# Differential attention's keys as pairs of the front, and query swaps by transfers inside SBUF, in a two-layer trunk step

## The chip, the cores and the metric

The kernel runs on one core of one Trainium2 chip. The metric is the device time of one execution in microseconds; the median of several runs counts. The profile is taken from one more execution.

## The reference

One inference step of a two-layer trunk for 128 prompt tokens and 512 sample tokens (640 columns in the kernel), model width 2048, in float32. Each layer: RMSNorm, shift and scale from a condition, one wide input projection whose column groups feed two mixers and their gates, one output projection, gated residual.

```python
def odd_mixer(h, w_in, w_out, cqn, ckn, c_lam, c_on, dqn, dkn, lam_init, ctx=None, rope=None):
    cq, ck, cv, cg, dq, dk, dv, dg = split_cols(h @ w_in, ODD_SPLIT)
    ...
    cq = rms_norm(cq.reshape(b, t, 2, C_HEADS, HEAD_DIM).transpose(0, 2, 3, 1, 4), cqn)
    ck = rms_norm(ck.reshape(b, t, 2, C_HEADS, HEAD_DIM).transpose(0, 2, 3, 1, 4), ckn)
    ...
    if ctx is None:
        ...
        new = (ck, cv, k_d, v_d)
    else:
        cos, sin = rope
        cq = apply_rope(cq, cos, sin)
        q_d = apply_rope(q_d, cos, sin)
        ck_all = jnp.concatenate([ctx[0], apply_rope(ck, cos, sin)], axis=3)
        ...
    o1 = attend(cq[:, 0][:, :, None], ck_all[:, 0], cv_all)[:, :, 0]
    o2 = attend(cq[:, 1][:, :, None], ck_all[:, 1], cv_all)[:, :, 0]
    o_c = rms_norm(o1 - lam.astype(o1.dtype) * o2, c_on) * (1.0 - lam_init)
    y_c = o_c.transpose(0, 2, 1, 3).reshape(b, t, C_W) * jax.nn.silu(cg)
    y_d = merge_heads(attend(q_d, dk_all, dv_all)) * jax.nn.silu(dg)
    return jnp.concatenate([y_c, y_d], axis=-1) @ w_out, new
```

Layer 1 (`odd_mixer`) has 4 heads of differential attention (C: two queries and two keys a head, 8 query and 8 key columns of 128, values of 256) and 8 query heads on 2 key heads of grouped attention (D). A key is normed by its row's RMS, scaled by a gain, and rotated by its position where it belongs to a sample token; 256 cached context keys go ahead of it. The normed prompt keys are an output as well. Layer 0 has banded grouped attention and a short convolution.

## The kernel before, in words

**Columns and products.** The input is held transposed: 16 tiles of 128 features x 640 tokens (`hs`), each as a high and a low part (float32r). A *column tile* is 128 columns of a weight matrix against all 640 tokens. Weights are loaded in quarters (4 x 128 rows, `load_raw`, on SP's queue), split into a high part by ScalarE and a low part by VectorE (`split_w`), and multiplied three times (high x high, high x low, low x high), in two halves of 320 tokens: 16 x 3 x 2 = 96 matmuls of 320 columns a tile.

**Tiles with work between them (`run_tiles`).** `slot` is called after each quarter, `pace_attn` after each half quarter. `prep` is a list of generators that finish a tile (each is advanced once a slot); `attn` is a queue of attention generators, of which only the first is advanced, by `steps / 2` at each of the eight calls in a tile (`brisk` holds `steps` by tile). `fill` is the modulation's product on VectorE, advanced `rate` times a slot (`FILL1`). Weights are loaded five quarters ahead and split three ahead (`RAW_AHEAD`, `SPLIT_AHEAD`). The program is written in this order; the order on each engine is made by the framework when it builds the kernel, and can differ (in the trace the scores of a step stand in the midst of a half quarter's matmuls).

**Pairs (`run_pairs`).** Two column tiles are multiplied together in seven products M1 to M7 in place of eight, from sums of weight blocks (VectorE: `sx`, `sf`) and of input blocks that are made once (`forms`): 7 x 8 x 3 = 168 matmuls of 320 columns a pair, and 14 weight splits of 128x512, where two plain tiles have 192 and 8. `begin` is called at a pair's start, `done` when a half of a tile is finished, `tail` in the last pair.

**Layer 1.** Its *front* (`project` with `h1_maker`, from about 1086 us to 1432 us) makes 14 gates, the 2 key tiles of D and the 10 value tiles of both mixers: six as plain tiles, twenty as ten pairs. Gates, keys and values go to HBM (`gdram`, `kdram`, `vdram`); values are transposed to rows ahead of that (`value_rows`), the two keys go raw. Then the pool `mid` is closed and `odd` opened, and a `run_tiles` of 26 tiles follows (the *mixers*, to about 2060 us): 8 queries of D, then for each of the four heads of C two queries and two keys, then two late gates. Attention runs between these tiles. `q_gen` finishes a query: it evicts it with its gain, copies four blocks of 32 partitions to swapped places (`qsw`, L751, on ScalarE), multiplies by cosines and sines, and sums squares on TensorE. `k_gen` finishes a key: transposes to rows, sums of squares (`junk`, L694), gain (L696, L699), the power -0.5 on GpSimd (L704), scaling (L707), rotation (L714 to L719), an output transfer, transposes back (L656) and splits, after `drain(attn)`. `keys_first` does it for D's keys, from their transfer back (`kx`, L684).

**One step of attention.** `pair_gen` (D) and `diff_gen` (C) alternate for each block of 128 queries: scores of the first query or map into PSUM (`S`, one buffer, L847 to L849), row maximum on VectorE (L809), its scaling (L811) and the exponential (L816) on ScalarE, then the second; transposes of the probabilities (L835), their splits, and the product with the values some steps later. A head of C has 15 steps. Keys and values have one buffer each, queries two.

Of the kernel before, what the change touches and what calls it, by code (L numbers as in the profile page):

```python
# [11 lines left out]
F32 = mybir.dt.float32  # L12
F32R = mybir.dt.float32r
# [7 lines left out]
P = 128  # L21
# [30 lines left out]
FILL1 = 0.85  # L52
# [4 lines left out]
def trunk_kernel(ctx: ExitStack, tc: tile.TileContext, I: dict, O: dict):  # L57
# [286 lines left out]
    prep, attn = [], []  # L344

# [324 lines left out]
    def k_gen(ap, pp, tag, src, gain, new_out, vals=None, then=None):  # L670

        vx = []

        def v_in(j):
            vx.append(ap.tile([P, 5, P], F32, tag="stg", name="vx", bufs=2))
            nc.sync.dma_start(vx[j].rearrange("p b f -> p (b f)"), vals[1][j])

        raw = ap.tile([P, 2, P], F32, tag="ctxk", name="ctxk", bufs=1)
        nc.sync.dma_start(raw, src.rearrange("(c p) d -> p c d", p=P))
        if isinstance(pp, tuple):  # L680
            x = stage(ap, pp)
        else:
            x = ap.tile([P, NT], F32, tag="stg", name="kx", bufs=2)
            nc.sync.dma_start(x, pp)  # L684
        if vals:
            v_in(0)
        yield
        ss = small.tile([P, 5], F32, tag="ss", name="ss")
        kg = ap.tile([P, 5, P], F32, tag="rp", name="kg", bufs=3)
        junk = ap.tile([P, P * st["sets"]], BF16, tag="junk", name="junk", bufs=1)[:, 0:P]  # L690
# [9 lines left out]
        if vals:  # L700
            v_in(1)
# [3 lines left out]
        yield  # L705
# [3 lines left out]
        m1 = ap.tile([P, 4, P], F32, tag="rp", name="m1", bufs=3)  # L709
        m2 = ap.tile([P, 4, P], F32, tag="rp", name="m2", bufs=3)  # L710
        x = kg[:, 0:4, :].rearrange("p b (a h f) -> p (b a) h f", a=2, h=2)
        y = m1.rearrange("p b (a h f) -> p (b a) h f", a=2, h=2)
        z = m2.rearrange("p b (a h f) -> p (b a) h f", a=2, h=2)
        V.tensor_mul(y, x, cosR[:, :, None, :].to_broadcast([P, 8, 2, 32]))  # L714
        yield
        V.scalar_tensor_tensor(out=z[:, :, 0, :], in0=x[:, :, 1, :], scalar=-1.0, in1=sinR,
                               op0=ALU.mult, op1=ALU.mult)
        V.tensor_mul(z[:, :, 1, :], x[:, :, 0, :], sinR)
        V.tensor_add(m1, m1, m2)  # L719
        yield  # L720
        drain(attn)
# [5 lines left out]
        split(hi[:, 0:CTX], lo[:, 0:CTX], t[:, 0:CTX])  # L727
        t = to_rows(lambda b: kg[:, b, :], False)
# [3 lines left out]
        if vals:  # L732
            yield
            hi, lo = st["v"] = tuple(ap.tile([P, 7, 2 * P], F32R, tag=t, name=t) for t in ("vh", "vl"))
            ctx_v(ap, vals[0], hi, lo, 2 * P)
            for j in range(2):
                cols = slice(j * P, (j + 1) * P)
                split(hi[:, 2:7, cols], lo[:, 2:7, cols], vx[j])
        if then:
            attn.append(then())  # L740


    def q_gen(ap, pp, tag, gain, then=None, wait=True):
# [5 lines left out]
        sw = ap.tile([P, NS], F32, tag="rp", name="qsw", bufs=3)  # L749
        for d in range(4):  # L750
            A.copy(sw[32 * d:32 * d + 32, :], x[32 * (d ^ 1):32 * (d ^ 1) + 32, 0:NS])  # L751
        yield
        m = ap.tile([P, NS], F32, tag="rp", name="qm", bufs=3)
        V.tensor_mul(m, x[:, 0:NS], cosT)
        V.tensor_mul(sw, sw, sinT)
        V.tensor_add(m, m, sw)
# [6 lines left out]
        if wait:  # L763
            yield
        t = psT()
# [108 lines left out]
    def pair_gen(ap, width, k, v, qs, banded, begin, emit, done, sinks):  # L874
# [38 lines left out]
        for u in range(7):  # L913
            if u >= 2:
                weigh(u - 2, [0, 2])
                groups(u - 2, [4])
            if u < 5:
                score(u, 0)
            yield
            if u >= 2 and len(plan(u - 2)[4]) > 4:  # L920
                weigh(u - 2, [4])
            if u < 5:
                score(u, 1)
            if 1 <= u < 6:
                groups(u - 1, [0, 2])
            if u < 6:
                yield
        done()
# [24 lines left out]
    kdram = [dram.tile([P, NT], F32, name=f"kd{k}") for k in range(2)]  # L953
# [4 lines left out]
    st = {"sets": 1}  # L958
# [580 lines left out]
    def odd_start():  # L1539
        ap = pools["cur"]  # L1540
        lam4 = ap.tile([P, 4, P], F32, tag="rp", name="lam4", bufs=3)
        nc.sync.dma_start(lam4, I["c_lambda"][0].rearrange("a d -> (a d)").partition_broadcast(P)
                          .rearrange("p (a d) -> p a d", a=4))
        lp = ap.tile([P, 2, P], F32, tag="rp", name="lp", bufs=3)
# [17 lines left out]
    def diff_gen(ap, h, v, kq):  # L1562
# [66 lines left out]
        for u in range(8):  # L1629
            if u >= 3:  # L1630
                out(u - 3)
            if 2 <= u < 7:
                weigh(u - 2)
            if u < 5:
                score(u, 0)
            if u == 7:
                break
            yield
            if u >= 2:
                norm(u - 2)  # L1640
            if u < 5:
                score(u, 1)
            if 1 <= u < 6:
                groups(u - 1)
            yield
# [31 lines left out]

    def key_out(j):
        x = xr_tile("kx")

        def put(t, sl, src):
            A.copy(x[:, sl], src)
            if (j, "k") in half_done:
                nc.gpsimd.dma_start(kdram[j], x)
            half_done.add((j, "k"))
        return put
# [7 lines left out]

    def front_begin(p):
        for t in range(2):
            n = N_FRONT + 2 * p + t
            m = n - len(FRONT)
            outs[t] = gate_out(n) if m < 0 else key_out(m) if m < 2 else value_out((m - 4) if m > 3 else m + 6)

    def front_done(p, t, h, src):
        outs[t](("sq", "acc")[t], HV[h][1], src)

    def front_tail(name):

        if name == "M7":
# [8 lines left out]
    project(I["od_w_in"][0], [(OD["cg"] + i * P) if i < 8 else OD["dg"] + (i - 8) * P for i in FRONT]  # L1715
            + [OD[n] + i * P for n, m in (("dk", 2), ("dv", 2), ("cv", 8)) for i in range(m)], N_FRONT, h1_maker,
            front_job, front_begin, front_done, front_tail, by_half=True)
    nc.sync.dma_start(tables, I["k_tables"])
    close("mid")
    open_pool("odd")  # L1720
    odd_start()
# [10 lines left out]
    st["sets"] = 2  # L1732
# [8 lines left out]
    def keys_first():  # L1741
        for kv in range(2):
            yield from k_job(f"k{kv}", I["cache_d_k"][0, 0, kv], "d_k_norm", O["new_d_k"][0, 0, kv])(kdram[kv])

    def in_twos(g):
        while next(g, DONE) is not DONE and next(g, DONE) is not DONE:
            yield

    def behind(g):
        yield  # L1750
        yield from g

    keys = keys_first()
    next(keys)
    prep.append(behind(in_twos(keys)))
    for h in range(4):
        for m in range(2):
            jobs.append((OD["cq"] + (m * 4 + h) * P, q_job(f"q{m}", "c_q_norm")))
        for m in range(2):
            more = (None, diff_then(h)) if m else ((I["cache_c_v"][0, 0, h], vdram[2 * h:2 * h + 2]),)  # L1760
            jobs.append((OD["ck"] + (m * 4 + h) * P,
                         k_job(f"k{m}", I["cache_c_k"][0, 0, m, h], "c_k_norm", O["new_c_k"][0, 0, m, h], *more)))

    brisk = {len(jobs): 1.75, len(jobs) + 1: 1.75}
    brisk.update((i, 1.6 if i < 11 else 1.1) for i in range(2, len(jobs)))
    for i in (4, 5):
        jobs.append((OD["cg"] + i * P, very_late_gate(i, (("rp", 3), ("stg", 2), ("rp", 3)))))
# [5 lines left out]
    def y1_maker(k):  # L1773
# [6 lines left out]
        else:  # L1780

            tag, n = (("q0h", 2), ("q0l", 2), ("q1h", 2), ("q1l", 2))[k] if k < 4 else (("rp", 3), ("stg", 2))[k % 2]
# [100 lines left out]
```

## Time and profile before

| | |
|---|---|
| median of 3 runs | 2266.32 us (2265.68 to 2266.66) |
| the profiled execution's own time | 2267.87 us |
| its span, first to last instruction | 2265.9 us |
| mean granted TensorE clock | 0.996 |
| TensorE matmul busy / weight load busy | 2221.5 us (98%) / 2148.4 us (95%) |
| VectorE / ScalarE / GpSimd busy | 1693.1 (75%) / 1167.9 (52%) / 223.5 us (10%) |

The profile's page gives busy times over the whole span. Matmuls are pipelined, so two records overlap and a mean of about 310 ns for a 320-column matmul is twice the time between two of them; windows with their instruction counts give that time. In rows of windows the columns are: stretch, its length, then busy us and (x instructions) of TensorE's matmuls, its weight loads, VectorE, ScalarE and GpSimd, the granted clock, the DMA share, and GB/s. In rows of groups: line, engine, operation, tiles written and read, shapes, count, then busy us, mean ns of one, idle time before and what ended it.

### The profile page before, as it was taken

To read this page: it belongs to the slowest core of one execution; us is meant where nothing else is said; L and a number is where in the kernel's file an instruction comes from. 1 tells how busy PE (TensorE), PEld (TensorE's weight loads), DVE (VectorE), ACT (ScalarE), POOL (GpSimd) and SP (SyncE) were. 2 spreads that over 40 slices of the span, in tenths; PEclk is the share of its full clock that TensorE was granted. 3 is DMA by queue.
4 is the path that set the end of the run, shared out by engine and by line. 5 is a ranking of instruction groups with operands and counts; after the bars stand their busy time and mean duration, and the time that the engine had idled before them with its cause. 6 is when DMAs were issued, how large, how long until landed. Compare 5 with 4: busy or idle time off the path is not lost.

```text
span 2265.9 us, 41110 instructions
## 1 busy us (share of the span) xinstructions
PE 2221.5 (98%) x15660; PEld 2148.4 (95%) x15660; DVE 1693.1 (75%) x2981; ACT 1167.9 (52%) x2473; POOL 223.5 (10%) x341
## 2 busy tenths in 40 slices
PE   7999999999999999999999999999999999999999
PEld 5889999999999999999999999899999999999999
DVE  4659898988888978877876666585766786576765
ACT  4335554645344445444744445577775666664443
POOL 2221101000100100000200000100001111111010
PEclk9999999999999999999999999999999999999999
DMA  9985556565453426753763333432424343246541
GB/s 357 330 287 173 160 167 198 173 188 161 154 156 113 150 85 219 218 148 106 261 200 108 117 110 112 151 103 70 124 84 140 96 132 111 83 134 224 166 135 45
DMA packets 377189, 354.03 MB, mean 156 GB/s; under 512 B 17170, under 2 KB 324848, under 8 KB 376480
## 3 DMA queue, kind: packets, MB, share of 16 engines
q1 hardware_dynamic: 360272, 291.07, 42.1%
q0 software_dynamic: 15856, 58.11, 7.3%
q8 instruction: 123, 2.02, 0.4%
q10 hardware_dynamic: 864, 2.23, 0.3%
q14 instruction: 74, 0.61, 0.1%
HBM read 307.17 MB, written 44.17 MB: 155 GB/s over the span
## 4 chain that ended last, share of the span: by engine, by line
PE 83%; DMA 4%; issue 4%; ACT 3%; DVE 3%; POOL 1%; SPq 1%; POOLq 0%; DVEq 0%; ACTq 0%
PE pq L626 10%; PE pq L628 10%; PE pq L627 10%; PE pa L332 6%; PE pa L333 6%; PE pb L332 6%; PE pa L334 6%; PE pb L333 6%; PE pb L334 6%; PE T L835 2%; PE S L847 2%; PE S L849 1%; PE S L848 1%; PE T L178 1%; DMA ada<-in_ada_w 1%
## 5 line engine op out<-in xcount | busy, mean ns | idle before, releaser
L297 ACT ACTIVATE wh<-raw 128x512 fp32r<-128x512 f32 (+1 forms) x388 | 233.2, 602 | 343.4 <-PE pb L333 227.4
L332 PE MATMUL pa<-h,wh 128*128 128x320 f32 x1152 | 367.7, 319 | 0.6 <-DVE sum L425 0.4
L332 PE MATMUL pb<-h,wh 128*128 128x320 f32 x1152 | 360.4, 313 | 0.9 <-ACT h L297 0.9
L333 PE MATMUL pa<-h,wh 128*128 128x320 f32 x1152 | 359.4, 312 | 0.9 <-DVE h L298 0.9
L334 PE MATMUL pa<-h,wl 128*128 128x320 f32 x1152 | 358.3, 311 | 0.0
L333 PE MATMUL pb<-h,wh 128*128 128x320 f32 x1152 | 357.8, 311 | 0.0
L334 PE MATMUL pb<-h,wl 128*128 128x320 f32 x1152 | 357.8, 311 | 0.0
L298 DVE TENSOR_TENSOR wl<-raw,wh 128x512 fp32r<-128x512 f32 (+1 forms) x388 | 253.5, 654 | 110.7 <-ACT wh L297 99.7
L626 PE MATMUL pq<-h,wh 128*128 128x320 f32 x960 | 297.7, 310 | 0.0
L627 PE MATMUL pq<-h,wh 128*128 128x320 f32 x960 | 296.6, 309 | 0.0
L628 PE MATMUL pq<-h,wl 128*128 128x320 f32 x960 | 296.4, 309 | 0.0
L332 PEld LDWEIGHTS pa<-h,wh 128*128 128x128 f32 x1152 | 217.4, 189 | 13.8 <-issue 12.5
L626 PE MATMUL pq<-T,wh 128*128 128x320 f32 x720 | 223.3, 310 | 0.0
L333 PEld LDWEIGHTS pa<-h,wh 128*128 128x128 f32 x1152 | 217.6, 189 | 5.9 <-issue 4.5
L628 PE MATMUL pq<-T,wl 128*128 128x320 f32 x720 | 222.6, 309 | 0.3 <-DVE wl L298 0.3
L627 PE MATMUL pq<-T,wh 128*128 128x320 f32 x720 | 222.4, 309 | 0.0
L332 PEld LDWEIGHTS pb<-h,wh 128*128 128x128 f32 x1152 | 217.2, 189 | 2.1 <-ACT h L297 1.1
L334 PEld LDWEIGHTS pa<-h,wl 128*128 128x128 f32 x1152 | 217.2, 189 | 2.1 <-issue 2.1
L333 PEld LDWEIGHTS pb<-h,wh 128*128 128x128 f32 x1152 | 217.5, 189 | 0.0
L334 PEld LDWEIGHTS pb<-h,wl 128*128 128x128 f32 x1152 | 217.2, 189 | 0.2 <-DVE wl L298 0.2
L297 ACT ACTIVATE wh<-sx 128x512 fp32r<-128x512 f32 x180 | 112.7, 632 | 154.5 <-PE pq L627 106.5
L251 DVE SCALAR_TENSOR_TENSOR acc<-adaw,sT,acc 128x1024 f32<-128x1024 f32 x150 | 189.3, 1278 | 0.0
(389 smaller groups left out, 4782.4 us busy)
## 6 DMA issues: line engine op xcount, KB each, us to landing
adaw<-in_ada_w SPq DMA_DIRECT2D x80, 512.0 KB, 3.9
raw<-in_od_w_in SPq DMA_DIRECT2D x148, 256.0 KB, 3.0
raw<-in_ev_w_in SPq DMA_DIRECT2D x130, 256.0 KB, 3.4
ada<-in_ada_w SPq DMA_DIRECT2D x11, 2048.0 KB, 12.7
adaw<-in_ada_w SPq DMA_DIRECT2D x64, 256.0 KB, 2.7
w<-in_od_w_in SPq DMA_DIRECT2D x30, 512.0 KB, 3.9
w<-in_ev_w_in SPq DMA_DIRECT2D x27, 512.0 KB, 3.7
adah<-in_ada_w SPq DMA_DIRECT2D x20, 512.0 KB, 9.2
```

The lines of the kernel that those rows point to most:

```text
L178: PE.matmul(acc[32 * g:32 * g + 32, 0:wd], sT[:, kt, :], w[:, kt % m, :], start=(i < 4), stop=(i >= KT - 4), tile_position=(0, 32 * g))
L251: V.scalar_tensor_tensor(out=acc[c], in0=w, scalar=sT[:, kt, c:c + 1], in1=acc[c], op0=ALU.mult, op1=ALU.add)
L297: A.activation(hi, x, AF.Copy)
L298: V.tensor_sub(lo, x, hi)
L332: PE.matmul(ps, wh[:, i, :], hi[:, sl], start=(j == js[0] if alone else (pos == 0 and j == 0)), stop=False)
L333: PE.matmul(ps, wh[:, i, :], lo[:, sl], start=False, stop=False)
L334: PE.matmul(ps, wl[:, i, :], hi[:, sl], start=False, stop=(j == js[1] - 1 if alone else (pos == 3 and j == 3)))
L626: PE.matmul(ps, wh[:, j, :], hi, start=(first and h == 0 and j == 0), stop=False, skip_group_check=True)
L627: PE.matmul(ps, wh[:, j, :], lo, start=False, stop=False, skip_group_check=True)
L628: PE.matmul(ps, wl[:, j, :], hi, start=False, stop=(final and h == 1 and j == 3), skip_group_check=True)
L835: PE.transpose(t[:, i * P:(i + 1) * P], p, ident)
L847: PE.matmul(d, q[0][:, bs], k[0][:, ks], start=True, stop=False)
```

## The change

The eight key tiles of C become four more pairs of the front, between D's keys and the values: the front then has 34 tiles, 28 of them as 14 pairs, and the mixers 18 tiles. All ten keys are finished in the front (`key_chain`: normed, scaled, written out, rotated, transposed back) and go to `kdram` finished. The rotation's row tables are loaded at the start of the front's pairs. `k_gen` is kept for layer 0 alone. In the mixers a head's two keys, its context and its values are loaded and split by `head_back`, which waits, by advancing attention, until the earlier heads' scores (`passed["scores"]`) and values have been used. The swapped query blocks are moved by four transfers on SP's queue in place of four ScalarE copies, in both layers, and multiplied by the sines one wait later. `FILL1` and the paces change; tag `rp` has two buffers in place of three in the pool `odd`, and a new tag `kk` has one.

```diff
-FILL1 = 0.85
+FILL1 = 1.1
...
+    passed = {"scores": 0, "values": 0}
...
     def q_gen(ap, pp, tag, gain, then=None, wait=True):
...
         for d in range(4):
-            A.copy(sw[32 * d:32 * d + 32, :], x[32 * (d ^ 1):32 * (d ^ 1) + 32, 0:NS])
+            nc.sync.dma_start(sw[32 * d:32 * d + 32, :], x[32 * (d ^ 1):32 * (d ^ 1) + 32, 0:NS])
         yield
...
         V.tensor_mul(m, x[:, 0:NS], cosT)
-        V.tensor_mul(sw, sw, sinT)
-        V.tensor_add(m, m, sw)
...
         if wait:
             yield
+        V.tensor_mul(sw, sw, sinT)
+        V.tensor_add(m, m, sw)
...
+    def key_chain(j, t):
+        yield
+        x, (gain, new_out) = st[t], KEYS[j][1:3]
+        ss = small.tile([P, 5], F32, tag="ss", name="ss")
+        kg = xr_tile("kg").rearrange("p (b f) -> p b f", b=5)
+        junk = pS.tile([P, 1024], F32, tag="S", name="sqj")[:, 0:P]
+        r = key_rows(x, ss, kg, junk, gains[gain])
+        yield
+        yield
+        m1 = x[:, 0:NS].rearrange("p (b f) -> p b f", b=4)
+        key_scale(kg, r, new_out, m1, cosF)
+        yield
+        m2 = xr_tile("m2")
+        key_turn(kg, m1, m2[:, 0:NS].rearrange("p (b f) -> p b f", b=4), sinF)
+        yield
+        yield
+        A.copy(m2[:, SPLIT], to_rows(lambda b: kg[:, b, :], False))
+        A.copy(m2[:, 0:NS], to_rows(lambda b: m1[:, b, :], True))
+        nc.gpsimd.dma_start(kdram[j], m2)
+        busy.discard(t)
...
     def front_begin(p):
+        if p == 0:
+            nc.sync.dma_start(tables[:, 3 * HALF:3 * HALF + 512], I["k_tables"][:, 0:512])
...
+    def key_load(j, tag, bufs):
+        ap = pools["cur"]
+        raw = ctx_keys(ap, KEYS[j][3])
+        x = ap.tile([P, NT], F32, tag=tag, name="kx", bufs=bufs)
+        nc.sync.dma_start(x, kdram[j])
+        return raw, x
+
+    def key_split(tag, raw, x):
+        hi, lo = new_keys(pools["cur"], tag, raw)
+        split(hi[:, CTX:], lo[:, CTX:], x)
...
     def keys_first():
...
+        key_split("k0", *first)
+        yield
+        second = key_load(1, "kk", 1)
+        yield
+        yield
+        key_split("k1", *second)
...
+    def head_back(h, n):
+        ap = pools["cur"]
+        k = key_load(2 + 2 * h, "kk", 1)
+        yield
+        yield
+        wait_for("scores", n)
+        key_split("k0", *k)
+        k = key_load(3 + 2 * h, "kk", 1)
+        craw = ap.tile([P, 2, 2 * P], F32, tag="ctxv", name="ctxv", bufs=1)
+        nc.sync.dma_start(craw, I["cache_c_v"][0, 0, h].rearrange("(c p) d -> p c d", p=P))
+        yield
+        key_split("k1", *k)
+        vx = [ap.tile([P, 5, P], F32, tag="stg", name="vx", bufs=2) for _ in range(2)]
+        for j in range(2):
+            nc.sync.dma_start(vx[j].rearrange("p b f -> p (b f)"), vdram[2 * h + j])
+        yield
+        wait_for("values", n)
...
+        attn.append(diff_then(h)())
...
     for h in range(4):
-        for m in range(2):
-            jobs.append((OD["cq"] + (m * 4 + h) * P, q_job(f"q{m}", "c_q_norm")))
-        for m in range(2):
-            more = (None, diff_then(h)) if m else ((I["cache_c_v"][0, 0, h], vdram[2 * h:2 * h + 2]),)
-            jobs.append((OD["ck"] + (m * 4 + h) * P,
-                         k_job(f"k{m}", I["cache_c_k"][0, 0, m, h], "c_k_norm", O["new_c_k"][0, 0, m, h], *more)))
+        jobs.append((OD["cq"] + h * P, q_job("q0", "c_q_norm")))
+        jobs.append((OD["cq"] + (4 + h) * P, last_q(h)))
 
-    brisk = {len(jobs): 1.75, len(jobs) + 1: 1.75}
-    brisk.update((i, 1.6 if i < 11 else 1.1) for i in range(2, len(jobs)))
+    brisk = {len(jobs): 2.0, len(jobs) + 1: 2.0}
+    brisk.update((i, 1.6 if i < 9 else 2.0) for i in range(2, len(jobs)))
```

`key_rows`, `key_scale` and `key_turn` hold the lines of `k_gen` from L685 to L719 unchanged in their work; `last_q` finishes a head's second query and starts `head_back`.

156 lines of the change are left out of this document (88 added, 68 removed).

## Prediction

> **What bounds the kernel now.** I read the page first, then the stages one by one in windows, because a share over the whole span mixes stages with different limits.
>
> ```profile
> span 2265.9 us, 41110 instructions
> PE 2221.5 (98%) x15660; PEld 2148.4 (95%) x15660; DVE 1693.1 (75%) x2981; ACT 1167.9 (52%) x2473; POOL 223.5 (10%) x341
> PE 83%; DMA 4%; issue 4%; ACT 3%; DVE 3%; POOL 1%; SPq 1%; POOLq 0%; DVEq 0%; ACTq 0%
> ```
>
> TensorE holds 83% of the chain that ended last; nothing else holds more than 4%. So what the change does to TensorE's own work counts first, and then how often TensorE is left waiting.
>
> ```profile
> core 0: us, PE busy (x) PEld busy (x) DVE busy (x) ACT busy (x) POOL busy (x), PEclk, DMA share, GB/s
> 300.00:420.00 120.00, 118.98 (x858) 113.92 (x857) 107.15 (x174) 57.25 (x135) 8.28 (x8) 1.00 0.58 177
> 656.00:880.00 224.00, 223.66 (x1532) 222.18 (x1532) 190.49 (x302) 101.21 (x177) 12.96 (x24) 1.00 0.40 121
> 1120.90:1148.90 28.00, 28.00 (x193) 28.00 (x192) 24.11 (x45) 15.71 (x27) 3.25 (x6) 1.00 0.76 231
> 1205.40:1303.90 98.50, 98.50 (x674) 98.50 (x673) 67.71 (x101) 45.55 (x84) 4.34 (x8) 1.00 0.38 115
> 1329.10:1432.10 103.00, 103.00 (x715) 102.96 (x714) 64.29 (x93) 53.75 (x108) 8.69 (x17) 1.00 0.35 109
> 1432.00:1700.00 268.00, 260.96 (x1822) 248.09 (x1821) 181.02 (x333) 191.81 (x411) 24.07 (x25) 0.99 0.36 108
> 1700.00:2004.00 304.00, 299.27 (x2105) 288.16 (x2104) 209.28 (x406) 183.21 (x489) 42.42 (x68) 1.00 0.38 115
> ```
>
> Two plain column tiles (192 matmuls) take 28.00 us in the third row, four pairs of the front (three of gates and the first keys', 4 x 168 = 672 matmuls) 98.50 us in the fourth, four value pairs, which transpose as well, 103.00 us in the fifth. Each way a 320-column matmul comes every 0.146 us, at the full granted clock, with no gap. The last two rows are layer 1's mixers, query attention first and differential attention from 1700: here tiles alternate with attention, and TensorE does wait. Whom its weight loads wait for, from 1432 on:
>
> ```profile
> engine line waited for: us in total, times, longest us
> PEld S L847 <- ACT p L816: 8.8, 21, 1.9
> PEld T L656 <- ACT ls L1549: 2.5, 1, 2.5
> PEld T L656 <- ACT kg L707: 2.0, 2, 1.4
> PEld T L656 <- DVE k1l L298: 1.9, 3, 1.4
> PEld T L1622 <- DVE kg L696: 1.3, 3, 0.6
> ```
>
> The first row is the one score tile (S, one buffer): the next scores wait until the last exponential has read it. The other four belong to the key chain: transposes waiting for the first key rows to be loaded, for the scaling of kg, or for a transpose bank held by the keys' splits.
>
> **The matmuls removed.** Eight key tiles of 96 matmuls leave the mixers, four pairs of 168 join the front: 768 - 672 = 96 fewer at 98.50 us / 672 = 0.1466 us, that is **-14.1 us**. This lies wholly on TensorE. The 100 key transposes only move: ten per value pair make (103.00 - 98.50) / 4 = 1.1 us, so a key pair with twenty costs 24.6 + 2.2 = 26.8 us, and the mixers lose as much.
>
> **The key chain moved into the front.** Per key it brings these instructions (means in ns); the swap's row and the weights' split stand with them:
>
> ```profile
> L696 DVE TENSOR_TENSOR kg<-T,gain_rows 128x512 f32<-128x512 f32 x12 | 8.3, 690 | 6.4 <-ACT junk L694 6.3
> L699 DVE TENSOR_TENSOR kg<-T,gain_rows 128x128 f32<-128x128 f32 x12 | 3.4, 281 | 0.0
> L714 DVE TENSOR_TENSOR m<-kg,tables 128x512 f32<-128x512 f32 x12 | 8.3, 692 | 20.2 <-ACT kg L707 20.2
> L716 DVE SCALAR_TENSOR_TENSOR m<-kg,tables 128x256 f32<-128x256 f32 x12 | 5.0, 419 | 0.0
> L718 DVE TENSOR_TENSOR m<-kg,tables 128x256 f32<-128x256 f32 x12 | 5.0, 419 | 0.0
> L719 DVE TENSOR_TENSOR m<-m,m 128x512 f32<-128x512 f32 x12 | 8.3, 688 | 0.2
> L707 ACT ACTIVATE kg<-kg,r 128x128 f32<-128x128 f32 x60 | 19.0, 391 | 18.4 <-POOL r L704 18.4
> L694 ACT ACTIVATE junk<-T 128x128 bf16<-128x128 f32 x60 | 16.6, 277 | 5.0 <-PE T L656 3.6
> L694 ACT ACTIVATION_READ_ACCUMULATOR junk<-T 128x1 f32 x60 | 11.7, 195 | 0.0
> L751 ACT COPY qsw<-qx 32x512 f32<-32x512 f32 x96 | 59.3, 618 | 1.6
> L298 DVE TENSOR_TENSOR wl<-raw,wh 128x512 fp32r<-128x512 f32 x340 | 233.5, 687 | 99.9 <-ACT wh L297 88.9 <-PE T L656 5.2 <-PE T L900 1.4
> ```
>
> VectorE: 690 + 281 + 692 + 419 + 419 + 688 = 3.19 us a key. A value pair has 64.29 / 4 = 16.1 us of VectorE; with two keys it is 22.5 us in 26.8, or 84%. The nearest row with that load is 656 to 880 above, nine pairs at 190.49 / 224 = 85%, and TensorE ran there without a gap (223.66 of 224): cover enough. ScalarE: 53.75 / 4 = 13.4 us for a value pair, plus ten squares with their accumulator (0.472 each) and ten scalings (0.391), 8.6 us: 22.0 of 26.8, or 82%. No row has ScalarE that full. Lower end 0; upper end one run of five squares, 2.4 us, late in each of the five key pairs: 12 us. I take **+1 us**, nearer to the gapless pair rows. GpSimd gets twenty transfers and twenty small operations more in a stage where it is busy 4.34 of 98.50 us; nobody but the chain itself waits for them.
>
> **The waits that go.** The four key rows above sum to 7.7 us. In the changed kernel the key needs only its two context transposes on TensorE; the finished key arrives by transfer and is split by ScalarE and VectorE alone. I take **-7 us** (ends -2, since a bank may be held by something else, and -8).
>
> **Denser differential attention.** By the pacing constants a head gets 8 steps a tile instead of 4.4, so that its 15 steps fit two tiles. Two things tighten. First VectorE: from the window 1700 to 2004 take away eight tiles (8 x 14.0 us) and 80 transposes (80 x 0.11) of time, 304 - 112 - 9 = 183 us, and of VectorE 32 splits at 0.687 and eight keys at 3.19, 209.28 - 22.0 - 25.5 = 161.8 us: 88%, against 69% now (the modulation fill in it is about as much as before). The row 300 to 420 has 107.15 / 120 = 89% with banded attention between tiles, and TensorE's waits there come to about 1 us. Second, the score chain, seen near the end of the mixers where the pace is already 7 steps a tile:
>
> ```profile
> 2007.53 0.97 ACT L816 ACTIVATE p<-S,nm,rq 128x768 f32<-128x768 f32 x1
> ...
> 2008.41 0.18 ACT L816 ACTIVATION_READ_ACCUMULATOR p<-S,nm,rq 128x1 f32 x1
> ...
> 2008.64 0.19 PEld L847 LDWEIGHTS S<-k0h,q0h 128*128 128x128 f32 x1 [0.17 <-ACT p L816]
> ...
> 2009.65 0.34 PE L849 MATMUL S<-k0h,q0l 128*128 128x384 f32 x1
> ...
> 2010.02 0.96 DVE L809 TENSOR_REDUCE nm<-S 128x1 f32<-128x768 f32 x1
> ...
> 2011.59 0.28 ACT L811 ACTIVATE nm<-nm,rq 128x1 f32<-128x1 f32 x1
> ```
>
> Last score matmul, maximum, scaling, exponential, accumulator: 0.34 + 0.96 + 0.28 + 0.97 + 0.18 = 2.7 us before the bank is free; the twelve matmuls between two steps cover 12 x 0.1466 = 1.8 us. The wait was 0.17 us here all the same, since the program's order on TensorE puts other matmuls of the tile ahead of the scores. Between map 0 and map 1 of a dense block there are 4 x 4 = 16 such crossings. Lower end 0; upper end the longest wait of the S row, 1.9 us, at each: 30 us. I take **+6 us**, 0.4 us each, the mean of that row (8.8 / 21).
>
> The same part adds waits. Key splits wait until the previous head's scores are done, and behind them on ScalarE lie weight splits; the second key's load waits on SP for the buffer of the first, ahead of weight loads. By the step count the scores end at step 10 of 15 and the first split comes about four steps later: nothing, with cover of some 10 us.
>
> **The query swap.** 96 copies of 0.618 us leave ScalarE (59.3 us, none of it a bound), 96 transfers join SP's queue.
>
> ```profile
> L684 SPq DMA_DIRECT2D kx<-kd x2: 377/394/411, 1439.7 to 1440.2; - x2
> DMA to landing us min/median/max: 2.4/4.4/5.8
>   ACT qsw L751: 15.6, 15
> SPq L310 <- DVE wl L298: 499.7, 222, 14.5
> ```
>
> Four issues of 0.39 us and a landing of 2.4 to 5.8 us (rows of the key load, five times the size) make 4 to 7 us instead of 2.5; the product with the sines now stands two slots later, 7 us or more, and VectorE loses the 15.6 us that it sat idle for the copies. I take 0, between -4 us (a quarter of that idle time) and +8 us (half a us at each of 16 queries in layer 1). The Trainium skill, DMA: Bandwidth & Descriptors, section Anatomy of one DMA, puts the fixed cost at about 2.0 us and the rest at bytes over 436 GB/s, an estimate of 2.2 us for 64 KB; the sum by it would be the same, as either lies inside the two slots.
>
> **The sum.** -14.1 + 1 - 7 + 6 + 0 = -14.1 us on the profiled execution's 2267.87 us: 2253.8. That execution is 1.55 us above the median of the runs, 2266.32, so I predict **2252 us**.
>
> **Rivals.** (1) *The score chain becomes the bound of differential attention*: each of the 16 crossings waits 1.9 us, 30 us in place of 6, and the total is 2276 us, slower. It decides from 20 us, 1.25 us a crossing (14.1 + 7 - 1). For it: 2.7 us against 1.8 us of cover, and VectorE, one link, at 88%. Against it: the mean of 0.4 us at almost that pace. Half-way it gives about 2266, no change. (2) *ScalarE late in the key pairs*: 12 us in place of 1, 2263 us. Against it: the weight splits run three half-products ahead. (3) *SP stands in line*: the swaps wait at SP's head for the query's eviction, and weight and modulation loads wait behind; 8 us, 2260 us. SP already stood 499.7 us ahead of weight loads without TensorE waiting for them. The Trainium skill, same page and section, says that any semaphore wait happens on the issuing sequencer before dispatch; by that rule the loads behind do wait, as the last row shows, and the price stays the one above. (4) *The saving isn't there*: excluded for the 96 matmuls, but the 7 us may only change their name: 2259 us.
>
> **Chances.** A measurement of this kernel can tell about 0.2%, 4.5 us, from no change. Forecast, own range 2245 to 2261: 0.56. Rival 1 in full 0.17, half-way 0.09; rival 2 0.06; rival 3 0.06; rival 4 0.06. Rivals 3 and 4 are still faster, by 6 and 7 us: 0.68 faster. Within 0.2% are rival 2 and rival 1 half-way, 0.15; slower 0.17. The range takes rival 1 as far as 4 us short of its full price: 2243 to 2272.
>
> **What would show it.** Right: 96 fewer wide matmuls; front pairs with keys at 26.8 us; the mixers' L656 waits for kg and kx gone; S waits 8 to 16 us; VectorE near 88% in differential attention. Wrong: S waits over 25 us, key pairs over 28 us, or weight splits that wait for raw loads.

## The result, and the profile after

The changed kernel takes **2251.77 us** (median of four runs, 2249.84 to 2256.83); the kernel before, run beside it on the same chip, 2266.49 us (2265.68 to 2269.07). The ratio is 0.9939, with a 95% interval of 0.9927 to 0.9952: faster by 14 us. The forecast was 2252. The profiled execution, 2249.84 us long, is the fastest of the four; it lies 18.0 us under the profiled execution before, where the medians differ by 14.7, so some 3 us of what follows from the two profiles belong to these executions and not to the change.

From the page of the changed kernel, the span, the engines and the chain that ended last:

```profile
span 2248.0 us, 41180 instructions
PE 2208.3 (98%) x15564; PEld 2133.0 (95%) x15564; DVE 1729.8 (77%) x3027; ACT 1131.9 (50%) x2423; POOL 230.1 (10%) x349
PE 83%; DMA 5%; issue 4%; DVE 4%; ACT 3%; POOL 2%; SPq 0%; ACTq 0%; POOLq 0%; DVEq 0%
```

The count of TensorE's instructions fell by 96, as the diff says, and its busy time by 13.2 us. The shares are what they were: a page of shares doesn't tell these two kernels apart. Stages do. The same four stages in both kernels (start to the first pair of layer 1's front; the front's pairs; the mixers up to the first pair of output tiles; the rest), before and then after, in columns of time, busy time with instructions for each engine, granted clock, DMA share and GB/s:

```profile
0.00:1180.80 1180.80, 1156.96 (x8279) 1110.64 (x8280) 963.20 (x1702) 555.49 (x1114) 115.42 (x176) 1.00 0.61 191
1180.80:1432.20 251.40, 251.40 (x1728) 251.35 (x1728) 164.99 (x242) 122.81 (x237) 15.36 (x29) 1.00 0.36 110
1432.20:2131.60 699.40, 683.41 (x4763) 657.43 (x4763) 478.27 (x900) 435.07 (x1019) 79.73 (x117) 1.00 0.41 126
2131.60:2265.90 134.30, 129.78 (x897) 129.00 (x895) 86.61 (x137) 54.56 (x104) 12.95 (x20) 1.00 0.31 93
```

```profile
0.00:1179.70 1179.70, 1157.54 (x8278) 1111.67 (x8279) 963.77 (x1702) 536.12 (x1082) 113.15 (x176) 1.00 0.61 194
1179.70:1546.50 366.80, 363.02 (x2501) 360.33 (x2500) 255.17 (x390) 204.77 (x491) 40.80 (x66) 1.00 0.35 107
1546.50:2113.80 567.30, 558.01 (x3895) 532.01 (x3895) 424.22 (x798) 336.44 (x747) 63.17 (x88) 1.00 0.49 151
2113.80:2248.00 134.20, 129.75 (x896) 128.96 (x894) 86.60 (x137) 54.56 (x104) 12.93 (x20) 1.00 0.32 93
```

The front's pairs grew by 115.4 us. Four pairs at 24.6 and a hundred transposes at 0.112 make 98.5 + 11.2 = 109.7; the other **5.7 us** are new waits. The mixers shrank by 132.1 us. Eight tiles of 96 matmuls at 0.1466 and the hundred transposes make 112.6 + 11.2 = 123.8; another **8.3 us** went with them. With the 1.1 us of the first row and 0.1 of the last: -1.1 - 14.1 + 5.7 - 8.3 - 0.1 = -17.9.

Where the 5.7 us are is seen in the waits of the five key pairs, 1303 to 1444 us (waiting engine, operation and line, what ended the wait: us, times, longest):

```profile
PEld T L657 <- DVE sq L703: 3.3, 5, 0.7
PEld T L657 <- issue: 3.0, 5, 0.6
PE T L657 <- DVE sq L703: 2.0, 5, 0.4
PE T L657 <- DVE acc L703: 1.8, 5, 0.4
```

Five pairs, two keys each: the first transpose of each finished key's rotated rows back to columns stands until VectorE's last addition of the rotation (L703) has ended, about half a microsecond with its weight load. (`sq` and `acc` are the tiles that hold the two keys' rotated rows; "issue" means that the profile shows nothing that the engine waited for.) The windows of those pairs, of the part of layer 0 that the prediction quotes, and of differential attention:

```profile
300.00:420.00 120.00, 118.98 (x858) 114.07 (x857) 107.06 (x175) 52.82 (x125) 7.68 (x8) 1.00 0.59 184
1303.40:1443.40 140.00, 136.22 (x942) 133.58 (x941) 106.06 (x170) 92.59 (x269) 27.41 (x42) 1.00 0.34 104
1780.00:1990.00 210.00, 205.63 (x1433) 192.42 (x1432) 175.41 (x340) 133.29 (x325) 30.40 (x45) 1.00 0.47 144
```

A key pair takes 140.0 / 5 = 28.0 us, 26.8 having been forecast. VectorE is busy 106.06 of 140 (76%) and ScalarE 92.59 (66%): neither is full, the transposes are simply asked for before the addition has ended. In differential attention VectorE reaches 175.41 / 210 = 84%. Whom the weight loads wait for in the mixers, 1547 to 2068:

```profile
PEld S L846 <- ACT p L815: 8.4, 30, 1.1
PEld T L756 <- issue: 3.1, 12, 0.7
PEld pa L332 <- issue: 2.9, 7, 0.4
PEld T L1624 <- DVE on L1619: 2.1, 3, 1.0
```

The rows of the key chain are gone. The score tile's row is as large as before (8.8 then), spread over more and shorter waits: 30 against 21, the longest 1.1 us against 1.9. Last, the swap: the transfers, then VectorE's product with the sines, its idle time ahead of it and the time to landing; and from SP's own waits the two largest of the swap and the one on weight buffers:

```profile
L750 SPq DMA_DIRECT2D qsw<-qx x96: 507/584/1506, 185.3 to 1962.8; - x96
  DMA qsw<-qx: 5.0, 5
DMA to landing us min/median/max: 1.9/2.1/5.1
```

```profile
SPq L310 <- DVE wl L298: 360.0, 188, 14.2
SPq L750 <- ACT q0h L297: 17.7, 8, 6.0
SPq L750 <- ACT q1h L297: 11.2, 5, 3.3
```

VectorE sits idle 5.0 us in all for the swapped query, where it had been 15.6 for the copies. SP does stand with swaps at its head, but its waits for weight buffers fell from 499.7 to 360.0 us: it is still far ahead.

### The profile page after: what moved, and what is told of

It reads as the page before. It is cut to its first block, busy times and chain, and to the rows that moved or that the text cites. A ratio compares the mean times of both kernels' runs of the same rounds, so it can differ in the third digit from the quotient of the medians.

```text
span 2248.0 us, 41180 instructions
## 1 busy us (share of the span) xinstructions
PE 2208.3 (98%) x15564; PEld 2133.0 (95%) x15564; DVE 1729.8 (77%) x3027; ACT 1131.9 (50%) x2423; POOL 230.1 (10%) x349
## 4 chain that ended last, share of the span: by engine, by line
PE 83%; DMA 5%; issue 4%; DVE 4%; ACT 3%; POOL 2%; SPq 0%; ACTq 0%; POOLq 0%; DVEq 0%
PE pq L627 11%; PE pq L628 11%; PE pq L629 11%; PE pa L332 6%; PE pa L333 6%; PE pb L332 6%; PE pa L334 6%; PE pb L333 6%; PE pb L334 6%; PE T L834 2%; PE S L846 2%; PE S L848 1%; PE S L847 1%; PE T L178 1%; PE T L897 1%
## 5 line engine op out<-in xcount | busy, mean ns | idle before, releaser
L627 PE MATMUL pq<-h,wh 128*128 128x320 f32 x1088 | 338.1, 311 | 0.0
L628 PE MATMUL pq<-h,wh 128*128 128x320 f32 x1088 | 336.2, 309 | 0.0
L629 PE MATMUL pq<-h,wl 128*128 128x320 f32 x1088 | 335.9, 309 | 0.0
L332 PE MATMUL pa<-h,wh 128*128 128x320 f32 x1024 | 325.7, 318 | 0.2 <-DVE sum L426 0.2
L332 PE MATMUL pb<-h,wh 128*128 128x320 f32 x1024 | 321.0, 314 | 0.9 <-ACT h L297 0.9
L333 PE MATMUL pa<-h,wh 128*128 128x320 f32 x1024 | 319.2, 312 | 0.6 <-DVE h L298 0.6
L333 PE MATMUL pb<-h,wh 128*128 128x320 f32 x1024 | 317.7, 310 | 0.0
L334 PE MATMUL pa<-h,wl 128*128 128x320 f32 x1024 | 317.4, 310 | 0.0
L298 DVE TENSOR_TENSOR wl<-raw,wh 128x512 fp32r<-128x512 f32 (+1 forms) x364 | 236.9, 652 | 92.0 <-ACT wh L297 87.9
L627 PE MATMUL pq<-T,wh 128*128 128x320 f32 x816 | 253.8, 311 | 0.0
L628 PE MATMUL pq<-T,wh 128*128 128x320 f32 x816 | 252.0, 309 | 0.0
L627 PEld LDWEIGHTS pq<-h,wh 128*128 128x128 f32 x1088 | 204.3, 188 | 0.8 <-issue 0.8
L628 PEld LDWEIGHTS pq<-h,wh 128*128 128x128 f32 x1088 | 204.4, 188 | 0.0
L332 PEld LDWEIGHTS pa<-h,wh 128*128 128x128 f32 x1024 | 192.4, 188 | 12.5 <-issue 11.6
L629 PEld LDWEIGHTS pq<-h,wl 128*128 128x128 f32 x1088 | 204.2, 188 | 0.0
L333 PEld LDWEIGHTS pa<-h,wh 128*128 128x128 f32 x1024 | 192.6, 188 | 6.0 <-issue 4.9
L332 PEld LDWEIGHTS pb<-h,wh 128*128 128x128 f32 x1024 | 193.1, 189 | 2.1 <-ACT h L297 1.1
## 6 DMA issues: line engine op xcount, KB each, us to landing
ada<-in_ada_w SPq DMA_DIRECT2D x11, 2048.0 KB, 13.5
```

The lines of the kernel that those rows point to most:

```text
L298: V.tensor_sub(lo, x, hi)
L332: PE.matmul(ps, wh[:, i, :], hi[:, sl], start=(j == js[0] if alone else (pos == 0 and j == 0)), stop=False)
L333: PE.matmul(ps, wh[:, i, :], lo[:, sl], start=False, stop=False)
L334: PE.matmul(ps, wl[:, i, :], hi[:, sl], start=False, stop=(j == js[1] - 1 if alone else (pos == 3 and j == 3)))
L627: PE.matmul(ps, wh[:, j, :], hi, start=(first and h == 0 and j == 0), stop=False, skip_group_check=True)
L628: PE.matmul(ps, wh[:, j, :], lo, start=False, stop=False, skip_group_check=True)
```

## Experiments

Every ratio is to the kernel before, run beside it (2267.9 to 2268.4 us), with its 95% interval; "lost against the change" is the difference of two ratios times 2267 us. Each interval reaches 2 to 3.5 us to either side, so such a difference is known to some 3.5 to 4.5 us. The mixers and fronts compared below come from one profiled execution of each kernel, whose time lies up to some 4 us from the median of its kernel's runs.

**The pairs undone.** All fourteen gates as plain tiles, the eight key tiles still in the front as pairs: the 96 matmuls come back, the rest of the change stays.

```
-    N_FRONT = 6
+    N_FRONT = 14
```

> The changed kernel with eight of the front's tiles as plain tiles again (fourteen plain gates, twenty columns as ten pairs); the keys are still pairs and still finished in the front, everything else is as changed. Theory A (the gain is the 96 matmuls that four pairs save, the other effects about cancel): 14 us are given back, 2265 to 2268 us, level with the kernel before. Rival B (the gain comes from the waits removed in the mixers and the denser pace, the pairs matter little): at most 6 us are given back, 2252 to 2258 us.

Measured: 2264.06 us, 0.9986 [0.9977, 0.9994]: 10.6 us lost against the change. Its front (from the start of layer 1's front to the first mixer tile) and its mixers, and the same front of the changed kernel below:

```profile
1083.90:1558.40 474.50, 467.82 (x3196) 464.50 (x3196) 292.55 (x479) 242.56 (x565) 54.19 (x91) 0.99 0.42 133
1558.40:2126.10 567.70, 558.38 (x3895) 532.03 (x3895) 424.37 (x798) 336.87 (x747) 62.84 (x87) 1.00 0.50 151
```

```profile
1085.50:1546.50 461.00, 453.74 (x3100) 450.39 (x3100) 332.03 (x535) 262.44 (x601) 54.10 (x90) 0.99 0.44 137
```

3196 instructions against 3100, and 13.5 us more, with the mixers as long as they were (567.7 and 567.3). So the term of -14.1 stands, by the profile to within a microsecond; the runs give less, 10.6, and the time lies 0.9 us under theory A's range and 6 over rival B's. Without this term all the rest of the change together gains 3 us.

**The transposes back one slot later.** The change, with a third wait in `key_chain`:

```
         yield
+        yield
         A.copy(m2[:, SPLIT], to_rows(lambda b: kg[:, b, :], False))
```

> The changed kernel with one more wait of a slot between a key's rotation and its transposes back in the front. Theory A (the ten waits of about 0.53 us, in which TensorE stands for the rotation's last addition, lie on the path): 4 to 6 us faster than the changed kernel, 2246 to 2248 us, and key pairs of 27 us in place of 28. Rival D (TensorE only changes what it waits for in those pairs, since VectorE is at 76% there and late anyway): no change, 2251 to 2253 us.

Measured: 2247.47 us, 0.9911 [0.9897, 0.9924], 6.4 us faster than the change. Four key pairs of it:

```profile
1332.10:1439.40 107.30, 107.30 (x755) 107.22 (x754) 83.34 (x136) 72.51 (x214) 22.05 (x34) 1.00 0.35 109
```

107.30 / 4 = 26.83 us a pair with no gap on TensorE, the 26.8 of the prediction; the profile shows no wait of its weight loads between 1303 and 1444. That is what theory A said: the waits of L657 cost TensorE their 5.7 us in full, and one slot's patience takes them away. This version is 20 us faster than the kernel before.

**The same in layer 0.** The version above, with one more wait ahead of the last transposes of `k_gen`, which layer 0 alone still uses:

```
         split(hi[:, CTX + NS:CTX + NT], lo[:, CTX + NS:CTX + NT], t)
+        yield
         t = to_rows(lambda b: m1[:, b, :], True)
```

> The changed kernel with the later transposes back in the front (as in the run before) and, in layer 0, one more wait of a slot ahead of a key's last transposes, which stood 2.7 and 1.2 us for a transpose bank that the context keys' split still held. Theory: 6 us for the front and 3 to 4 us for layer 0, together 9 us faster than the changed kernel, 2242 to 2246 us where the kernel before has 2267. Rival: the bank is held by other work one slot later as well, and only the front's 6 us are had, 2246 to 2249 us.

Measured: 2246.05 us, 0.9910 [0.9897, 0.9924]: by the ratio the same as without it, as the rival said; the 3 to 4 us of layer 0 didn't come. The wait that it was meant for, from 160 to 560 us, is the one the changed kernel has, to the digit:

```profile
PEld T L657 <- DVE k0l L298: 4.1, 2, 2.8
```

It names the key's lower half (L298), which holds the transpose bank; the rotation isn't late there. A remedy for one wait is not one for another on the same line.

**The swap by copies again.** The change with the four ScalarE copies in place of the transfers, everything else kept; and the reverse, the kernel before with the transfers and the later sines alone.

```
-            nc.sync.dma_start(sw[32 * d:32 * d + 32, :], x[32 * (d ^ 1):32 * (d ^ 1) + 32, 0:NS])
+            A.copy(sw[32 * d:32 * d + 32, :], x[32 * (d ^ 1):32 * (d ^ 1) + 32, 0:NS])
```

> The changed kernel with the query's swapped blocks copied by ScalarE again, as before; the product with the sines stays where the change put it. Theory A (the swap is hidden either way): within 2 us of the changed kernel, 2250 to 2254 us. Rival C (taking 59 us off ScalarE is what lets the denser attention keep up): 4 us or more slower, over 2256 us.

```
 (in the kernel before)
-            A.copy(sw[32 * d:32 * d + 32, :], x[32 * (d ^ 1):32 * (d ^ 1) + 32, 0:NS])
+            nc.sync.dma_start(sw[32 * d:32 * d + 32, :], x[32 * (d ^ 1):32 * (d ^ 1) + 32, 0:NS])
...
-        V.tensor_mul(sw, sw, sinT)
-        V.tensor_add(m, m, sw)
...
             yield
+        V.tensor_mul(sw, sw, sinT)
+        V.tensor_add(m, m, sw)
```

> The kernel before with the query swap alone done by transfers, and the sines one wait later. Theory A (hidden either way): within 2 us of the kernel before, 2264 to 2268 us. Rival C (ScalarE's relief counts by itself): 4 us or more faster, under 2262 us. Rival E (the swaps stand in SP's line ahead of weight loads): 4 us or more slower, over 2270 us.

Measured: with copies 2260.66 us, 0.9966 [0.9953, 0.9978], 6.1 us lost against the change; the transfers alone 2263.18 us, 0.9983 [0.9974, 0.9992], 3.9 us gained on the kernel before. Their mixers, first the change with copies, then the kernel before with transfers:

```profile
1546.00:2120.70 574.70, 559.01 (x3896) 531.35 (x3895) 423.97 (x798) 376.16 (x811) 60.23 (x87) 1.00 0.46 142
```

```profile
1433.70:2125.40 691.70, 678.87 (x4764) 654.45 (x4762) 478.11 (x900) 397.41 (x955) 79.84 (x117) 1.00 0.44 133
```

574.7 against 567.3 and 691.7 against 699.4: 7.4 and 7.7 us of the mixers in either setting. So theory A missed in the changed kernel, and 3.9 us in the kernel before lie between its range and rival C's. The prediction put the swap at nothing; it gives 4 to 6 us by the runs (the second edit moves the sines as well; no run moves those alone). The first row gives another thing: 574.7 - 699.4 = -124.7, and -112.6 - 11.2 of it are tiles and transposes. The rest, -0.9 us, is all that moving the keys and packing attention denser did to the mixers together, where -7 + 6 = -1 was forecast. That the two agree to 0.1 us is closer than two profiled executions can tell.

**Why the copies cost.** Is it that four in a row hold ScalarE for 2.5 us? The copies on ScalarE, spread over three slots:

```
+        def swap(d):
+            A.copy(sw[32 * d:32 * d + 32, :], x[32 * (d ^ 1):32 * (d ^ 1) + 32, 0:NS])
+        swap(0)
         yield
+        swap(1)
+        swap(2)
...
             yield
+        swap(3)
         V.tensor_mul(sw, sw, sinT)
```

> The changed kernel with the swap on ScalarE again, but its four copies spread over three slots (one, two, one) in place of four in a row. Theory F (the burst of 2.5 us ahead of the score chain's exponential is what costs): most of the 6 us are had, 2251 to 2255 us. Rival J (what costs is ScalarE's 40 us in the mixers, wherever they stand): as slow as with four in a row, 2258 to 2262 us.

Measured: 2260.47 us, 0.9964 [0.9951, 0.9976], as slow as in a burst, as rival J said; the mixers of its profile:

```profile
1544.40:2124.70 580.30, 561.28 (x3895) 533.16 (x3894) 423.48 (x798) 376.52 (x811) 61.14 (x87) 1.00 0.46 140
```

Taking the burst apart gains nothing. The last copy now stands right ahead of the product that needs it, but VectorE's idle time for the block is no larger for it, 12.3 us against 14.6 with four in a row. So the burst by itself isn't the reason.

Or is any place off ScalarE as good? The swap on GpSimd, `G.tensor_copy(` in place of `nc.sync.dma_start(`:

> The changed kernel with the swapped blocks copied by GpSimd in place of the transfers. Theory F (the swap gained because four copies in a row no longer hold ScalarE's queue, on which the exponential of the score chain stands): any place off ScalarE does it, within 3 us of the changed kernel, 2250 to 2256 us where the kernel before has 2267. Rival G (what helped was the transfers, or the sines one wait later): as slow as with ScalarE's copies, 2258 us or more.

Measured: 2275.16 us, 1.0032 [1.0021, 1.0042], 21 us lost against the change and slower than the kernel before. Its copies, and its mixers:

```profile
L750 POOL COPY qsw<-qx x96: 600/974/1667, 185.6 to 1990.0; 32x512 f32<-32x512 f32 x96
1558.40:2139.50 581.10, 561.26 (x3896) 533.53 (x3895) 434.47 (x798) 335.64 (x747) 113.56 (x151) 1.00 0.46 140
```

ScalarE is as free as with transfers (335.64 us), yet the mixers are 13.8 us longer: a copy takes 0.97 us at the median, not 0.62, and VectorE, which needs the block, waits behind all four. They also begin 11.9 us later (1558.4 for 1546.5), so nearly half of the loss lies in what comes before, all of it in the stretch of layer 0's own eight queries (160 to 572 us for 160 to 560). Neither theory foresaw a swap slower than ScalarE's. Who then waits, over the whole span:

```profile
  DVE qsw L762: 19.4, 18
  ACT q1h L297: 18.5, 9
  ACT q0h L297: 16.8, 9
```

With the transfers the three are 5.0, 5.0 and 12.1 us. So the late block passes its lateness on to VectorE and from there to ScalarE's split of the query (q0h, q1h). With ScalarE's copies VectorE's wait is only 4.8 us less, 14.6, and that kernel is 15 us faster; so that the lateness of the block is the whole cause is argued, not shown.

**Where TensorE waits for it.** In the mixers TensorE's weight loads and matmuls wait at the score tile, with the transfers (the row of the weight loads is above), with ScalarE's four copies, with the spread copies and with GpSimd's:

```profile
PE S L846 <- ACT p L815: 1.8, 3, 0.8
```

```profile
PEld S L846 <- ACT p L815: 13.4, 30, 1.2
PE S L846 <- ACT p L815: 6.3, 12, 0.9
```

```profile
PEld S L850 <- ACT p L819: 13.0, 30, 2.0
PE S L850 <- ACT p L819: 5.5, 10, 1.7
```

```profile
PEld S L846 <- ACT p L815: 14.4, 30, 2.0
PE S L846 <- ACT p L815: 7.3, 10, 1.8
```

Together 10.2, 19.7, 18.5 and 21.7 us: in the changed kernel every copied swap goes with exponentials that free the score tile later. It isn't the whole of it, since in the kernel before these waits are 12.7 us with copies and 11.5 with transfers, while the mixers there shorten by 7.7.

Does a fuller ScalarE cost as such? The change with four idle copies (32 x 384, onto themselves, of no use to the result) beside each of layer 1's swaps:

```
             nc.sync.dma_start(sw[32 * d:32 * d + 32, :], x[32 * (d ^ 1):32 * (d ^ 1) + 32, 0:NS])
+            if st["rp"] == 2:
+                A.copy(gain_rows[32 * d:32 * d + 32], gain_rows[32 * d:32 * d + 32])
```

> The changed kernel, swaps by transfers, with four idle copies of 32x384 on ScalarE per query of layer 1, in place, of a table that nothing reads any more, at the spot where the swap's copies stood: some 32 us of ScalarE's time that nothing waits for. Theory J (ScalarE's time in the mixers costs TensorE, wherever it stands): 3 to 6 us slower than the changed kernel, 2255 to 2258 us. Rival K (what the transfers saved was the wait of the products on the copies, not ScalarE's time): under 2 us slower, 2250 to 2254 us.

Measured: 2264.58 us, 0.9985 [0.9975, 0.9995], 10.4 us lost, more than either theory said. It answers another question than the one asked, because nothing ties an idle copy to its query, and the program's order put all 64 of them into one stretch:

```profile
L752 ACT COPY gain_rows<-gain_rows x64: 495/510/515, 1427.0 to 1484.9; 32x384 f32<-32x384 f32 x64
1427.00:1485.00 58.00, 49.83 (x312) 48.87 (x311) 29.80 (x45) 55.13 (x113) 4.81 (x9) 0.91 0.31 97
PE T L657 <- ACT sq L1680: 7.3, 2, 3.9
```

That is the front's last key pair and the first value pairs, with ScalarE full at 55.13 of 58 us, TensorE busy 49.83 at a granted clock of 0.91, and its transposes waiting for an eviction (L1680). The mixers, 567.4 us, are as in the changed kernel. So a full ScalarE among pairs does stall TensorE here; the changed kernel, at 66% in its key pairs, is far from it. On the copies in the mixers the run says nothing, and that question stays open.

**The density of differential attention.** Rival 1 said that the score chain would become the bound. Lengthen the chain, then, by two idle 128 x 1 ScalarE copies in layer 1 (they do nothing to the values), in the change and in the kernel before:

```
             A.activation(nm, nm, AF.Copy, scale=rsc)
+            A.copy(nm, nm)
+            A.copy(nm, nm)
```

> The changed kernel with two idle copies of 128x1 on ScalarE after the scaling of every row maximum in layer 1, so that the score chain is 0.58 us longer at each of the 64 dense scores. Rival 1 (the score chain is the bound): 64 x 0.58 = 37 us slower than the changed kernel, near 2290 us. Theory A (TensorE waits for it only now and then): 5 to 12 us slower, 2257 to 2266 us. Fully covered: under 2 us.

> The kernel before with the same two idle copies in every score chain of layer 1. Theory A (the slower pace of differential attention covers the chain there; the grouped attention's pace is the same in both): 2 to 7 us slower than the kernel before, less than half of what the changed kernel loses. If the score chain tells as much here, the denser pace took no cover away.

Measured: on the change 2258.74 us, 0.9948 [0.9932, 0.9963], 2.0 us lost; on the kernel before 2274.48 us, 1.0028 [1.0017, 1.0038], 6.4 us lost. In the traces the time from the start of the scaling to the start of the exponential, on the mean of the 64 dense scores, grew from 0.40 to 1.03 us in the change and from 0.50 to 1.26 in the kernel before. A chain that was the bound would have passed its whole lengthening on, 64 x 0.63 = 40 us; neither kernel comes near. The 2.0 us are less than theory A's 5 to 12. The order of the two is the opposite of what was expected, but the 4.4 us between them are no more than such differences are known to, and the mixers of the profiled change are 7.3 us longer than without the copies (574.6 us for 567.3). So whether the denser pace took cover away isn't settled by these two runs.

The pace itself, slowed for the tiles from number 9 on:

```
-    brisk.update((i, 1.6 if i < 9 else 2.0) for i in range(2, len(jobs)))
+    brisk.update((i, 1.6) for i in range(2, len(jobs)))
```

> The changed kernel with 6.4 attention steps a tile in differential attention in place of 8 (the pace of grouped attention kept to the end); eight steps are then forced in a row at the places that wait for the earlier head. Theory A (the denser pace costs waits, about 5 us of them): fewer score waits but the forced steps stand without cover, within 4 us of the changed kernel. If density were the main cost: 5 us or more faster. If the pace of 8 is needed to hide the attention: 5 us or more slower.

Measured: 2253.31 us, 0.9931 [0.9918, 0.9945]; mixers 569.0 us. No change that the runs can tell, so density between these two paces neither costs nor gains more than some 4 us. The score waits didn't become fewer, as theory A had it: 10.4 us of weight loads and 4.4 of matmuls, 14.8 for 10.2.

And VectorE, the engine that is busy 84% in differential attention: the modulation fill computed on one column in place of its whole width (15 of 16 of its products are left out).

```
-                        V.scalar_tensor_tensor(out=acc[c], in0=w, scalar=sT[:, kt, c:c + 1], in1=acc[c],
+                        V.scalar_tensor_tensor(out=acc[c][:, 0:1], in0=w[:, 0:1], scalar=sT[:, kt, c:c + 1],
...
```

> The changed kernel with the modulation fill of the mixers computed on one column only after its first step (fifteen sixteenths of its products are left out, its loads stay): about 80 us of VectorE's time go. Theory A (VectorE's load costs TensorE little): 0 to 5 us faster than the changed kernel, 2247 to 2253 us. Rival H (VectorE at 88% is what most remaining waits come from): 8 us or more faster, under 2245 us.

Measured: 2254.41 us, 0.9932 [0.9917, 0.9948]. The mixers and the score row:

```profile
1545.90:2116.40 570.50, 559.43 (x3894) 533.59 (x3894) 366.92 (x798) 335.86 (x747) 61.31 (x88) 1.00 0.49 150
PEld S L846 <- ACT p L815: 13.2, 34, 2.5
```

VectorE has 57.3 us less to do in the mixers (424.22 before the edit) and the time doesn't move by more than the runs can tell; it lies 1.4 us over theory A's range and 9 over rival H's. The score row reads 13.2 us where the changed kernel has 8.4, in mixers 3 us longer (with the matmuls' row 18.8 for 10.2). All the rows of TensorE's waits in the mixers sum to 44.4 us for 40.6, so the others fell by some 5 us. One row is no measure of time lost: what TensorE waits at the score tile it need not wait elsewhere.

## Why the prediction was right, and where only its sum was

The total came out to 0.2 us, and that is partly luck: at least two terms were mis-sized, by about as much and with opposite signs.

- *The matmuls removed, -14.1*: right. 13.5 us in the front of the kernel with the pairs undone, 10.6 by the runs (known to some 3.5 us).
- *The key chain in the front, +1*: too small, **+5.7** by the profile and 6.4 by the runs. The step that failed is the reading "cover enough". It compared the load of VectorE and ScalarE with rows that ran without gaps, and the loads were no problem: 76% and 66% in pairs of 28.0 us, lower even than the 84% and 82% that it had added up for 26.8. What it didn't work out was the order of one chain: at which slot the transposes back are asked for, and when the rotation's addition ends. Key pairs of 28.0 us were on the list of what would show it wrong, at just that bound. Rival 2 saw that the key pairs could grow, at twice the price (12 us) and with the wrong cause: the late engine is VectorE, not ScalarE, and not by load but by position.
- *The waits that go, -7, and denser attention, +6*: right in sum as far as two profiles can tell, -0.9 in the mixers once the swap is by copies again. The key chain's rows did vanish. How the -0.9 splits isn't shown. In the changed kernel the score row is 8.4 us, inside the forecast 8 to 16, with VectorE at 84% for 88% foretold; but as the row can rise by 5 us with little in time, it proves neither term alone. That a slower pace gave nothing back speaks for a cost of density near zero, and then the waits that went are worth about -1 and not -7: two terms that were each too large and cancelled, which no run here separates.
- *The query swap, 0*: too small, **-3.9** alone and **-6.1** inside the change. The prediction saw two sides, a transfer's latency and VectorE's idle time of 15.6 us, took the quarter of the latter as the lower end, and then chose the middle. ScalarE's 59.3 us were put down as "none of it a bound". That it wasn't the bound is true, and it still cost; the burst of four copies isn't the reason. The transfers' own latency was well inside the two slots: 2.1 us to landing at the median (5.1 at most), 2.4 to 5.8 having been taken from a larger transfer. The Trainium skill, DMA: Bandwidth & Descriptors, section Anatomy of one DMA, gave an estimate of 2.2 us. The section states its figures for transfers that GpSimd issues, and these are issued on SP's queue; the trace's median of 2.1 us lies close to the estimate all the same.
- *Rival 1* (the score chain as the bound, 2276 us): refuted by the lengthened chain. *Rival 3* (SP in line): SP does wait at the swaps, 17.7 us in the largest row, but the weight splits wait about as long for raw loads as before (ScalarE 11.7 us for 10.3, on layer 0's first projection in both kernels); SP's slack of 360 us takes it. *Rival 4* (the waits only change their name, +7): the mixers' sum of -0.9 speaks against it only together with a cost of density, and that isn't shown; if density costs nothing, most of the forecast 7 us did stay under other names.

With the counted -14.1 for the matmuls, and from the timed runs +6.4 for the new waits and -6.1 for the swap, the sum is -13.8 us, and a ratio of 0.9939 takes 13.8 us off 2267. With the 10.6 us that the run of the pairs gave it would be -10.3. The sum closes, then, to within what the differences are known to.

**Left open**: by which way ScalarE's swap copies cost 4 to 6 us. Shown is that transfers take this cost away and that GpSimd's copies add to it; that it is the time at which the block is ready would fit both, but spread copies, the last of which stands a wait later, cost no more than a burst by the runs, and no run here delays the transfers by themselves. `FILL1` and the buffer counts weren't tried alone either; the sum leaves them no more than its own uncertainty.

## What to carry to other kernels

When a chain of small steps is moved under a dense stage, don't stop at the load of each engine: write down the slot in which every step is asked for and the one in which the step before it ends, since one `yield` too few cost 6 of 20 possible microseconds here at 76% load. Work on an engine that isn't the bound may still be worth taking away, as the 4 to 6 us of the swap show; an edit priced at zero between two ends deserves a run by itself. And a total that fits is no proof of its terms: undo the parts one at a time and see whether each gives back its own share.

## What the runs showed of the hardware that was not expected

- A transfer inside SBUF of 32 x 512 f32 (64 KB) lands after 2.1 us at the median (1.9 to 5.1); its issue on SP takes 0.58 us, against 0.39 for the key load of five times the size.
- GpSimd needs 0.97 us at the median (0.60 to 1.67) to copy the same block to other partitions, ScalarE 0.62; the swap on GpSimd cost 21 us against the transfers.
- Of VectorE's 424 us in the mixers 57 could be taken away without a gain in time that the runs can tell, at 75% load.
